# Splitting the attention of three token tiles around an expert gather, in a two-layer kernel on one Trainium2 core

## The chip, the cores and the metric

The kernel runs on one core of one Trainium2 chip. The metric is device time in microseconds (us) from the first to the last instruction of one execution, as the median of several runs. The core's engines are named as in the profile: PE is TensorE's matmul, PEld its weight load, DVE is VectorE, ACT is ScalarE, POOL is GpSimd, SP is SyncE; the core has 16 DMA engines, which SP's loads and POOL's gathers share.

## The reference

512 tokens of width 1024 in f32 pass through two layers. What matters here, cut down:

```python
def first_block(x, ...):
    h = rmsnorm(x, norm1_g)
    qa, ka, va, qb, kb, vb, ga, gb = split(h @ w_in)
    ya = neighbourhood_attention(qa, ka, va, rpb)      # 8 heads of 64
    yb = gqa_attention(rope(norm(qb)), rope(norm(kb)), vb)
    merged = sigmoid(ga) * (ya @ w_proj_a) + sigmoid(gb) * (yb @ w_proj_b)
    x = x + merged @ w_out
    x = x + peer(rmsnorm(x, norm2_g), peer_w_q, peer_sub_keys, peer_u, peer_v)
    return rmsnorm(x, norm_f_g)

def peer(xn, w_q, sub_keys, u, v):
    # per token: 8 heads, top 16 of 128 keys on two sides, top 16 of their sums:
    # 128 experts of 16384, each a row of u and a row of v
    act = einsum("cd,ced->ce", xc, u[ic])
    hid = gelu(act) * gate
    return einsum("ce,ced->cd", hid, v[ic])

def second_block(x, ...):      # a state-space layer over the sequence, in order
    ...
```

Each token picks 128 experts, and each expert is 8 KB (1024 values of u, 1024 of v). For 512 tokens that is 512 MB of rows read by index, against some 170 MB of weights.

## The kernel before

The tokens are four tiles of 128 (0 to 3), one token per partition. The order of work is written by hand and then list-scheduled by the framework, which keeps dependences.

**Front.** Keys and values of all tokens; then attention, gates and merge of tile 0 alone (`mix_first`), then tile 0's expert queries and choices (`queries`, `ranked`).

**The gather.** `peers` is a generator. One step of it handles two experts of the current tile (a pair). For each expert, POOL issues one indirect DMA that brings 128 rows of 8 KB (1 MB) into a buffer `g` (six buffers, line 269); DVE multiplies the u half with the token and sums it (L271); ACT applies gelu (L276); DVE puts act times gate on a diagonal `dg` (L280); PE multiplies `dg` with the v half, in 64 x 64 quarters of its array, into two accumulators (L285). For tile 0 both experts of a pair share one gelu and one visit of PE, PE takes only the left half of v, and DVE adds up the right half in a buffer `own` (L295). A tile has 64 pairs; the four tiles have 256. At the end of a tile `folded` adds the accumulators to the residual `xres` and leaves `pre[t]`.

**Beside it.** `Paced` wraps PE: each matmul counts its columns (times 4 for f32), and whenever the count passes `every`, one step of `peers` is emitted. So other PE work and gather pairs alternate: one pair per 13600 columns (`PACE_B`) during `mix_rest([1, 2, 3])` (attention, gates `ga`/`gb`, merge `pj`/`xo` of the other three tiles at once, with 384 columns per matmul) and during the queries of tile 1; one per 10500 (`PACE_Q`) during the queries of tiles 2 and 3; then the choices of tiles 2 and 3 on DVE, with `steps_now(3)` after each head; then, once tile 1 is folded, one per 4600 (`PACE_C`) during the second layer of tiles 0 and 1 (`block_c([0, 1])`). What is left of the gather is drained, and `block_c([2, 3])` ends the kernel.

**Choices.** `top8` and `best` find the experts on DVE. `best` writes the indices `hk_idx[t]`; a pair cannot be gathered before its indices exist. `rows` and `cols` load a weight tile of 512 KB from SP for every 8 matmuls of a stage, whatever the number of token columns; four such tiles are in flight (`wp`). The bias tables `nab` of the attention are loaded per call of `mixers`, as wide as its tiles need.

Of the kernel before, what the change touches and what calls it, by code (L numbers as in the profile page):

```python
# [8 lines left out]
F32 = mybir.dt.float32  # L9
# [5 lines left out]
OP = mybir.AluOpType  # L15
# [5 lines left out]
NT = 4  # L21
# [152 lines left out]
def program(tc, a, out):  # L174
# [3 lines left out]
    first, rest = [0], [1, 2, 3]  # L178
    NG = 256
    PACE_B, PACE_Q, PACE_C = 13600, 10500, 4600  # L180

    with ExitStack() as ctx:
# [40 lines left out]
        folds = [two[:, 1:3, :], two[:, 0:2, :]]  # L223
# [21 lines left out]

        def peers(gp, lp):
# [5 lines left out]
            for t in range(NT):  # L252
# [7 lines left out]
                for e0 in range(0, P, 2):  # L260
                    while len(hk_idx[t]) < e0 + 2:
                        yield
                    gs = []
                    grp = 2 if t == 0 else 1
                    for j in range(2):
                        if j % grp == 0:
                            act = sm.tile([P, 2], F32, tag="act", name="act", bufs=4)
                        g = gp.tile([P, 2, D], F32, tag="g", name="g")
                        G.indirect_dma_start(out=g.rearrange("p a d -> p (a d)"), out_offset=None, in_=a["uv"],  # L269
                                             in_offset=bass.IndirectOffsetOnAxis(ap=hk_idx[t][e0 + j], axis=0))  # L270
                        V.scalar_tensor_tensor(g[:, 0, :], g[:, 0, :], 1.0, xnp, op0=OP.mult, op1=OP.mult,  # L271
                                               accum_out=act[:, j % grp:j % grp + 1])
                        gs.append(g)
                        if (j + 1) % grp:
                            continue
                        A.activation(act[:, :grp], act[:, :grp], AF.Gelu)  # L276
                        gate = hk_gate[t][:, e0 + j + 1 - grp:e0 + j + 1]
                        dg = dgs()
                        for m in range(grp):
                            V.tensor_scalar(dg[:, m, :], two[:, 1, :], act[:, m:m + 1], gate[:, m:m + 1], op0=OP.mult, op1=OP.mult)  # L280
                        for m in range(2):
                            for i in range(2):
                                r, o = slice(64 * i, 64 * i + 64), slice(64 * m, 64 * m + 64)
                                w, v = (dg[r, m, :], gs[m][r, 1, HALVES[0]]) if grp == 2 else (dg[r, 0, :], g[r, 1, HALVES[m]])
                                T.tensor.matmul(acc[i][o, :], w, v, start=(e0 + j + 1 == grp), stop=(e0 + j + grp >= P),  # L285
                                                tile_position=(64 * i, 64 * m), skip_group_check=True)
                    if t == 0:
                        hid = sm.tile([P, 2], F32, tag="hid", name="hid", bufs=4)
                        V.tensor_tensor(hid, act, gate, op=OP.mult)
                        for j, g in enumerate(gs):  # L290
                            if own is None:
                                own = gp.tile([P, 512], F32, tag="own", name="own", bufs=1)
                                V.tensor_scalar(own, g[:, 1, HALVES[1]], hid[:, 0:1], None, op0=OP.mult)
                            else:
                                V.scalar_tensor_tensor(own, g[:, 1, HALVES[1]], hid[:, j:j + 1], own, op0=OP.mult, op1=OP.add)  # L295
                    if parts is not None:
                        folded(t - 1, parts, done[1])
                        parts = None
                    yield
                done = acc, own  # L300

            A.activation(col("rt"), act[:, 0:1], AF.Sqrt, bias=eps, scale=0.0)
# [11 lines left out]
        def folded(t, parts, own):  # L314

            acc = [bank("fold", "sb")] + ([bank("fold", "sb")] if own is None else [own])
            for i in range(2):
                if own is None:
                    for k in range(2):
                        r, o = slice(64 * k, 64 * k + 64), slice(64 * i, 64 * i + 64)  # L320
                        T.tensor.matmul(acc[k][o, :], two[r, 1, :], parts[r, i, :], start=True, stop=True,
                                        tile_position=(64 * k, 64 * i), skip_group_check=True)
                else:
                    T.tensor.matmul(acc[0], folds[i].rearrange("p a b -> p (a b)"), parts[:, i, :], start=(i == 0), stop=(i == 1))
# [3 lines left out]
            for k, h in enumerate(HALVES):  # L328
                V.tensor_tensor(xt[:, h], xt[:, h], acc[k], op=OP.add)
                A.activation(acc[k], xt[:, h], AF.Square, accum_out=ss[:, k, 0:1])  # L330
# [56 lines left out]
        with pool("pa") as pa:  # L387
# [28 lines left out]
            with pool("ph") as ph:  # L416
# [76 lines left out]
                def mix_rest(tiles, hs):  # L493
                    n = len(tiles) * P
                    with pool("p2") as py:
# [9 lines left out]
                        def spread(u):  # L505

                            if u < 8:
                                gate(u, a["wga"], mT)
                            if 12 <= u < 20:
                                if not gb:  # L510
                                    gb.append(pa.tile([P, 8, n], F32, tag="kv", name="gb"))
# [632 lines left out]
```

## Time and profile before

| | us |
|---|---|
| median of 3 runs | 2219.3 (2218.5 to 2221.38) |
| profiled execution, its own time | 2217.67 |
| its span | 2215.8 |
| PE busy | 1851.5 |
| DVE busy | 1628.1 |
| ACT busy | 735.1 |
| POOL busy | 598.8 |

The span runs from the first to the last instruction; 1.9 us lie around it. Busy times of engines overlap. The mean granted TensorE clock is 0.887. HBM reads are 707.67 MB. A window row of the profile gives, for a stretch in us from the span's start, the busy time of each engine, PE's granted clock, the DMA engines' mean busy share and the GB/s that they moved.

### The profile page before, as it was taken

Reading aid. Unit: us, or ns where it says so; the run is one execution under the profiler, and the core shown is the slowest. Engines: PE = TensorE matmul, PEld = TensorE weight load, DVE = VectorE, ACT = ScalarE, POOL = GpSimd, SP = SyncE. Lnnn points to the kernel's source line nnn. Section 1 sums busy time; section 2 is a strip of 40 time slices with the busy share of each in tenths; the row PEclk is TensorE's granted clock in tenths of the full one; section 3 lists DMA queues with packets and bytes.
Section 4 is the critical chain, followed back from the end, with each engine's and each line's share of the span. In section 5 each row is a group of like instructions: output and inputs, shape, how many; then the busy total and the mean of one; then the engine's idle time right before and its main releaser. Section 6 shows DMA issues by size and latency. Waiting matters only on the chain.

```text
span 2215.8 us, 29509 instructions
## 1 busy us (share of the span) xinstructions
PE 1851.5 (84%) x10292; PEld 1032.5 (47%) x10292; DVE 1628.1 (73%) x4007; ACT 735.1 (33%) x1471; POOL 598.8 (27%) x520
## 2 busy tenths in 40 slices
PE   7998699899999898656648886896899866799998
PEld 5767445444444654001104552462453421298896
DVE  5376986788885966888868887886775766687865
ACT  4374265566501421111123342321220310154443
POOL 0000223333331233444433334433423333200000
PEclk9999789999999998656758997998999976699999
DMA  5366979889997899999989989899999999653363
GB/s 211 127 228 216 363 288 344 335 325 350 346 381 273 316 378 394 380 380 397 362 306 346 418 365 396 335 418 420 406 415 416 402 416 421 276 170 97 119 189 121
DMA packets 127316, 711.71 MB, mean 321 GB/s; under 512 B 15168, under 2 KB 18752, under 8 KB 61248
## 3 DMA queue, kind: packets, MB, share of 16 engines
q0 software_dynamic: 73728, 536.90, 60.6%
q1 hardware_dynamic: 53440, 172.92, 22.1%
q8 instruction: 83, 1.36, 0.2%
q14 instruction: 65, 0.53, 0.1%
HBM read 707.67 MB, written 2.10 MB: 320 GB/s over the span
## 4 chain that ended last, share of the span: by engine, by line
PE 36%; DMA 25%; DVE 24%; issue 7%; ACT 6%; POOL 1%; another core or an unknown queue 0%; DVEq 0%; POOLq 0%; ACTq 0%; SPq 0%
DMA g<-in_uv,idx 23%; DVE g L271 9%; PE sc L168 5%; PE acc L285 4%; PE mix L168 3%; PE pq L168 2%; PE ga L168 2%; PE z L168 2%; DVE dg L280 2%; PE pg L168 2%; PE ys L168 2%; DVE ww L354 2%; POOL g L269 1%; DVE own L295 1%; PE xbc L168 1%
## 5 line engine op out<-in xcount | busy, mean ns | idle before, releaser
L269 POOL DMA_INDIRECT g<-in_uv,idx x512 | 595.0, 1162 | 1297.7 <-PE acc L285 610.2
L285 PE MATMUL acc<-g,dg 64*64 64x512 f32 x3584 | 626.5, 755 | 249.9 <-DVE dg L280 229.8
L271 DVE SCALAR_TENSOR_TENSOR g<-g,xnp 128x1024 f32<-128x1024 f32 x512 | 624.7, 1221 | 188.2 <-DMA g<-in_uv,idx 181.9
L285 PEld LDWEIGHTS acc<-g,dg 64*64 64x64 f32 x3584 | 122.9, 154 | 621.0 <-DVE dg L280 492.8
L276 ACT ACTIVATE act<-act 128x1 f32<-128x1 f32 (+1 forms) x448 | 90.8, 203 | 945.7 <-DVE g L271 912.2
L354 DVE TENSOR_TENSOR ww<-w,ww 128x1024 fp32r<-128x1024 f32 x175 | 213.4, 1222 | 76.4 <-ACT ww L353 74.5
L280 DVE TENSOR_SCALAR dg<-two,act,gate 128x64 f32<-128x64 f32 x512 | 172.1, 351 | 132.6 <-ACT act L276 129.9
L353 ACT CAST ww<-w 128x1024 fp32r<-128x1024 f32 x175 | 182.2, 1044 | 172.8 <-PE sc L168 63.6
L168 PEld LDWEIGHTS sc<-hT,ww 128*128 128x128 f32 x1536 | 190.0, 193 | 54.0 <-issue 44.5
L168 PE MATMUL sc<-hT,ww 128*128 128x256 f32 x1536 | 206.1, 289 | 6.0 <-ACT fold L333 3.2
L168 PE MATMUL pq<-xT,w 128*128 128x128 f32 (+1 forms) x768 | 127.8, 323 | 0.6 <-DMA w<-in_wq 0.6
L168 PEld LDWEIGHTS pq<-xT,w 128*128 128x128 f32 x768 | 112.0, 200 | 19.8 <-issue 12.2
L295 DVE SCALAR_TENSOR_TENSOR own<-g,hid,own 128x512 f32<-128x512 f32 x127 | 95.1, 749 | 2.3
L168 PE MATMUL ga<-h,w 128*128 128x384 f32 x256 | 93.1, 513 | 2.8 <-DVE rot L411 2.8
L276 ACT ACT_TABLE_LOAD x61 | 78.3, 1283 | 18.1 <-DVE g L271 16.3
L168 PE MATMUL xbc<-hT,ww 128*128 128x256 f32 x480 | 64.2, 290 | 6.2 <-DVE ww L354 3.3
L168 PEld LDWEIGHTS xbc<-hT,ww 128*128 128x128 f32 x480 | 59.3, 192 | 20.4 <-issue 9.5
L168 PEld LDWEIGHTS ga<-h,w 128*128 128x128 f32 x256 | 48.7, 198 | 37.6 <-issue 8.3
L168 PE MATMUL q<-h,w 128*128 128x128 f32 (+1 forms) x256 | 61.1, 394 | 3.4 <-ACT rsq L407 3.4
L168 PE MATMUL mix<-w,ycat 128*128 128x512 f32 x128 | 61.5, 612 | 0.0
L168 PEld LDWEIGHTS z<-hT,ww 128*128 128x128 f32 x384 | 46.9, 190 | 12.3 <-issue 10.5
L168 PE MATMUL z<-hT,ww 128*128 128x256 f32 x384 | 50.5, 287 | 1.5 <-ACT raw L928 1.3
(338 smaller groups left out, 2269.8 us busy)
## 6 DMA issues: line engine op xcount, KB each, us to landing
w<-in_w SPq DMA_DIRECT2D x100, 512.0 KB
w<-in_wq SPq DMA_DIRECT2D x48, 512.0 KB
w<-in_wo SPq DMA_DIRECT2D x32, 512.0 KB
w<-in_wgm SPq DMA_DIRECT2D x16, 512.0 KB
w<-in_wout SPq DMA_DIRECT2D x16, 512.0 KB
g<-in_uv,idx POOLq DMA_INDIRECT x512
w<-in_wpg SPq DMA_DIRECT2D x16, 512.0 KB
w<-in_wqa SPq DMA_DIRECT2D x8, 512.0 KB
```

The lines of the kernel that those rows point to most:

```text
L168: return self.count(max(n, 128) * (4 if rhs.dtype == F32 else 1), self.tensor.matmul(out, lhsT, rhs, **kw))
L269: G.indirect_dma_start(out=g.rearrange("p a d -> p (a d)"), out_offset=None, in_=a["uv"], in_offset=bass.IndirectOffsetOnAxis(ap=hk_idx[t] ...
L271: V.scalar_tensor_tensor(g[:, 0, :], g[:, 0, :], 1.0, xnp, op0=OP.mult, op1=OP.mult, accum_out=act[:, j % grp:j % grp + 1])
L276: A.activation(act[:, :grp], act[:, :grp], AF.Gelu)
L280: V.tensor_scalar(dg[:, m, :], two[:, 1, :], act[:, m:m + 1], gate[:, m:m + 1], op0=OP.mult, op1=OP.mult)
L285: T.tensor.matmul(acc[i][o, :], w, v, start=(e0 + j + 1 == grp), stop=(e0 + j + grp >= P), tile_position=(64 * i, 64 * m), skip_group_chec ...
L295: V.scalar_tensor_tensor(own, g[:, 1, HALVES[1]], hid[:, j:j + 1], own, op0=OP.mult, op1=OP.add)
L353: A.copy(ww[:, 0], w)
L354: V.tensor_tensor(ww[:, 1], w, ww[:, 0], op=OP.subtract)
```

## The change

`mix_rest` is called twice: for tiles 1 and 2, and later for tile 3. After the first call come the queries of tiles 1 and 2 together, with tile 1's choices made at once and tile 2's scores kept. After the second call come tile 3's queries. The choices of tiles 2 and 3 are a list `side` of small functions (one per head, one per `best` of four heads); `peers` runs one of them after every third pair. In `peers` each expert has its own gelu and its own visit of PE; for tile 0 PE takes both halves of v of every even expert and the left half of every odd one, and DVE adds up the right half of the odd ones only. The three paces change. The gates are spread over the attention units by a rule that depends on the number of tiles. The pools `pk` (choices) and the place of `gb` are new.

```diff
-    first, rest = [0], [1, 2, 3]
+    first, late = [0], [2, 3]
     NG = 256
-    PACE_B, PACE_Q, PACE_C = 13600, 10500, 4600
+    PACE_B, PACE_Q, PACE_C = 11300, 6400, 5200
...
-                for e0 in range(0, P, 2):
-                    while len(hk_idx[t]) < e0 + 2:
+                for e in range(P):
+                    while len(hk_idx[t]) <= e:
                         yield
-                    gs = []
-                    grp = 2 if t == 0 else 1
-                    for j in range(2):
...
-                        A.activation(act[:, :grp], act[:, :grp], AF.Gelu)
-                        gate = hk_gate[t][:, e0 + j + 1 - grp:e0 + j + 1]
-                        dg = dgs()
-                        for m in range(grp):
-                            V.tensor_scalar(dg[:, m, :], two[:, 1, :], act[:, m:m + 1], gate[:, m:m + 1], op0=OP.mult, op1=OP.mult)
-                        for m in range(2):
-                            for i in range(2):
-                                r, o = slice(64 * i, 64 * i + 64), slice(64 * m, 64 * m + 64)
-                                w, v = (dg[r, m, :], gs[m][r, 1, HALVES[0]]) if grp == 2 else (dg[r, 0, :], g[r, 1, HALVES[m]])
-                                T.tensor.matmul(acc[i][o, :], w, v, start=(e0 + j + 1 == grp), stop=(e0 + j + grp >= P),
-                                                tile_position=(64 * i, 64 * m), skip_group_check=True)
-                    if t == 0:
-                        hid = sm.tile([P, 2], F32, tag="hid", name="hid", bufs=4)
-                        V.tensor_tensor(hid, act, gate, op=OP.mult)
-                        for j, g in enumerate(gs):
...
-                                V.scalar_tensor_tensor(own, g[:, 1, HALVES[1]], hid[:, j:j + 1], own, op0=OP.mult, op1=OP.add)
...
+                    V.scalar_tensor_tensor(g[:, 0, :], g[:, 0, :], 1.0, xnp, op0=OP.mult, op1=OP.mult, accum_out=act)
+                    A.activation(act, act, AF.Gelu)
+                    dg = dgs()
+                    V.tensor_scalar(dg[:, 0, :], two[:, 1, :], act, hk_gate[t][:, e:e + 1], op0=OP.mult, op1=OP.mult)
+                    aside = t == 0 and e % 2 == 1
+                    for k in range(1 if aside else 2):
+                        for i in range(2):
+                            r, o = slice(64 * i, 64 * i + 64), slice(64 * k, 64 * k + 64)
+                            last = P - 2 if k and t == 0 else P - 1
+                            T.tensor.matmul(acc[i][o, :], dg[r, 0, :], g[r, 1, HALVES[k]], start=(e == 0), stop=(e == last),
+                                            tile_position=(64 * i, 64 * k), skip_group_check=True)
+                    if aside:
+                        hid = sm.tile([P, 1], F32, tag="hid", name="hid", bufs=4)
+                        V.tensor_tensor(hid, act, hk_gate[t][:, e:e + 1], op=OP.mult)
...
+                            V.scalar_tensor_tensor(own, g[:, 1, HALVES[1]], hid, own, op0=OP.mult, op1=OP.add)
+                    if e % 2:
+                        if parts is not None:
+                            folded(t - 1, parts, done[1])
+                            parts = None
+                        if side and e % 6 == 1:
+                            side.pop(0)()
+                        yield
...
-                            if u < 8:
-                                gate(u, a["wga"], mT)
-                            if 12 <= u < 20:
...
-                                gate(u - 12, a["wgb"], gb[0])
+                            each = 2 if len(tiles) == 1 else 1
+                            kind, v = divmod(u, 4 * len(tiles))
...
+                            for i in range(each * v, min(each * v + each, 8)):
+                                gate(i, a["wgb" if kind else "wga"], gb[0] if kind else mT)
...
                 T.beside(peers(gp, lp), PACE_B)
-                mix_rest(rest, h2)
-        late = rest[1:]
-        with pool("p4") as pw:
-            with pool("p5") as pq:
-                queries(pq, rest[:1], [(h, 2, rest[:1]) for h in (0, 2, 4, 6)], lambda *x: ranked(pw, *x))
-            T.every = PACE_Q
...
-            with pool("p5") as pq:
-                queries(pq, late, [(h, 2, late) for h in (0, 2, 4, 6)], after)
-
-            for t in late:
-                for h in range(8):
...
-                    T.steps_now(3)
-            while 1 not in pre:
-                T.steps_now(1)
-            T.every = PACE_C
+                mix_rest([1, 2], h2[:, :, 0:2 * P])
+                pk = pick.enter_context(pool("pk", side="right"))
...
+                def choices(t):
+
+                    for h in range(0, 8, MOST):
+                        f = []
+                        for m in range(MOST):
+                            side.append(lambda f=f, h=h, m=m: part(t, f, h, m))
+                        side.append(lambda f=f, h=h: best(pk, t, f, h, MOST))
+
+                with pool("p3") as pw:
+                    queries(pw, [1, 2], [(h, 2, [1, 2]) for h in (0, 2, 4, 6)], after)
+                T.every = PACE_Q
+                choices(2)
+                mix_rest([3], h2[:, :, 2 * P:])
+        with pool("p5") as pq:
+            queries(pq, [3], [(h, 2, [3]) for h in (0, 2, 4, 6)], after)
+        choices(3)
+        while side:
+            T.steps_now(1)
+        pick.close()
+        while 1 not in pre:
+            T.steps_now(1)
+        T.every = PACE_C
```

`after` ranks tile 1's heads at once and copies the scores of tiles 2 and 3 to a kept tile; `part` copies two rows of scores and runs `top8` on them. `folded` takes tile 0's second half as two 64 x 64 products more and one DVE addition of `own`.

## Rows read from the trace of the kernel before

**Rows 1.** The page: span, DMA busy tenths and GB/s in 40 slices, the ending chain by line.

```profile
span 2215.8 us, 29509 instructions
...
DMA  5366979889997899999989989899999999653363
GB/s 211 127 228 216 363 288 344 335 325 350 346 381 273 316 378 394 380 380 397 362 306 346 418 365 396 335 418 420 406 415 416 402 416 421 276 170 97 119 189 121
...
DMA g<-in_uv,idx 23%; DVE g L271 9%; PE sc L168 5%; PE acc L285 4%; PE mix L168 3%; PE pq L168 2%; PE ga L168 2%; PE z L168 2%; DVE dg L280 2%; PE pg L168 2%; PE ys L168 2%; DVE ww L354 2%; POOL g L269 1%; DVE own L295 1%; PE xbc L168 1%
```

**Rows 2.** Windows: stretch, its us, busy by engine (instructions), PE clock, DMA share, GB/s.

```profile
225.00:700.00 475.00, 427.83 (x1896) 208.41 (x1896) 380.60 (x969) 213.72 (x378) 147.27 (x127) 0.94 0.88 338
700.00:741.00 41.00, 39.78 (x305) 35.30 (x304) 24.03 (x142) 10.89 (x26) 1.51 (x2) 1.00 0.78 257
741.00:765.00 24.00, 14.41 (x69) 10.21 (x67) 19.41 (x95) 15.35 (x26) 4.21 (x6) 0.79 0.93 372
...
765.00:875.00 110.00, 101.49 (x572) 60.22 (x568) 70.14 (x211) 25.89 (x72) 39.53 (x35) 0.96 0.95 374
875.00:1135.00 260.00, 153.95 (x724) 25.31 (x728) 221.95 (x739) 38.67 (x135) 113.83 (x91) 0.63 0.95 377
1135.00:1215.00 80.00, 54.22 (x325) 26.92 (x318) 56.08 (x121) 20.46 (x53) 25.12 (x22) 0.80 0.85 317
1215.00:1780.00 565.00, 487.92 (x3040) 254.29 (x3042) 425.31 (x871) 157.53 (x347) 210.31 (x179) 0.93 0.99 400
1780.00:1915.00 135.00, 88.35 (x444) 16.60 (x436) 84.49 (x159) 13.60 (x56) 52.07 (x51) 0.72 1.01 419
```

**Rows 3.** Timeline of POOL, 676 to 765: gathers by start, us, idle before and releaser.

```profile
683.95 1.50 POOL L269 DMA_INDIRECT g<-in_uv,idx  x1 [0.30 <-issue]
...
739.19 0.94 POOL L269 DMA_INDIRECT g<-in_uv,idx  x1 [53.74 <-issue]
...
745.40 0.94 POOL L269 DMA_INDIRECT g<-in_uv,idx  x1 [0.30 <-issue]
764.90 0.94 POOL L269 DMA_INDIRECT g<-in_uv,idx  x1 [18.57 <-DVE idxf L789]
```

**Rows 4.** Groups by line, 225 to 700: count, busy us, mean ns, idle before, releasers.

```profile
L285 PE MATMUL acc<-g,dg 64*64 64x512 f32 x512 | 87.5, 650 | 23.6 <-DVE dg L280 22.9 <-DVE hid L289 0.7
...
L168 PE MATMUL pq<-xT,w 128*128 128x128 f32 x87 | 13.6, 323 | 0.0
L168 PE MATMUL sc<-subk,q 128*128 128x128 f32 x16 | 4.3, 384 | 2.6 <-ACT q L715 2.6
...
L295 DVE SCALAR_TENSOR_TENSOR own<-g,hid,own 128x512 f32<-128x512 f32 x127 | 95.1, 749 | 2.3
L276 ACT ACT_TABLE_LOAD x34 | 43.6, 1283 | 0.6
```

**Rows 5.** Groups by line and shape, the whole span: PE's query products.

```profile
L168 PE MATMUL pq<-xT,w 128*128 128x128 f32 x512 | 64.5, 284 | 0.6 <-DMA w<-in_wq 0.6
L168 PE MATMUL pq<-xT,w 128*128 128x256 f32 x256 | 63.3, 401 | 0.0
```

**Rows 6.** Windows of the gather's accumulators alone (PE, PEld, DVE, ACT).

```profile
765.00:875.00 110.00, 38.65 (x276) 8.76 (x272) 0.00 (x0) 0.00 (x0) 0.96 0.95 374
```

**Rows 7.** Timeline of PE, 333 to 339: start, us, instructions merged.

```profile
334.22 1.07 PE L285 MATMUL acc<-g,dg 64*64 64x512 f32 x4
335.22 0.66 PE L171 MATMUL pT<-idn,s 128*128 128x128 f32 x4
335.81 1.93 PE L285 MATMUL acc<-g,dg 64*64 64x512 f32 x12
```

**Rows 8.** Windows: a stretch with weights and gathers, one with gathers alone, one of choices.

```profile
1215.00:1315.00 100.00, 89.25 (x691) 60.09 (x693) 87.27 (x198) 40.17 (x81) 36.19 (x30) 1.00 1.02 419
...
1835.00:1895.00 60.00, 40.43 (x196) 6.74 (x192) 38.80 (x73) 4.86 (x24) 24.25 (x24) 0.68 1.01 421
...
975.00:1015.00 40.00, 23.83 (x116) 3.99 (x112) 35.97 (x123) 6.43 (x21) 17.34 (x13) 0.60 0.88 335
```

**Rows 9.** DMA queues: packets, MB, time of their packets as a share of 16 engines.

```profile
q0 software_dynamic: 73728, 536.90, 60.6%
q1 hardware_dynamic: 53440, 172.92, 22.1%
```

More of the change, by code (lines that the diff above doesn't have):

```diff
@@ L244, in program @@
         hk_idx, hk_gate, hk_f = {}, {}, {}
+        side = []
         def peers(gp, lp):
@@ L314, in folded @@
         def folded(t, parts, own):
-            acc = [bank("fold", "sb")] + ([bank("fold", "sb")] if own is None else [own])
+            acc = [bank("fold", "sb") for _ in range(2)]
             for i in range(2):
[L318 to L324, printed above, removed]
+                for k in range(2):
+                    r, o = slice(64 * k, 64 * k + 64), slice(64 * i, 64 * i + 64)
+                    T.tensor.matmul(acc[k][o, :], two[r, 1, :], parts[r, i, :], start=True, stop=True,
+                                    tile_position=(64 * k, 64 * i), skip_group_check=True)
             xt = xres[:, t, :]
@@ L329, in folded @@
                 V.tensor_tensor(xt[:, h], xt[:, h], acc[k], op=OP.add)
+                if k and own is not None:
+                    V.tensor_tensor(xt[:, h], xt[:, h], own, op=OP.add)
                 A.activation(acc[k], xt[:, h], AF.Square, accum_out=ss[:, k, 0:1])
@@ L505, in spread @@
                         def spread(u):
[L507 to L512 removed]
+                            each = 2 if len(tiles) == 1 else 1
+                            kind, v = divmod(u, 4 * len(tiles))
+                            if kind and not gb:
+                                last = tiles[-1] == NT - 1
+                                gb.append((pa if last else py).tile([P, 8, n], F32, tag="kv" if last else "gb", name="gb"))
+                            for i in range(each * v, min(each * v + each, 8)):
+                                gate(i, a["wgb" if kind else "wga"], gb[0] if kind else mT)
                         def put(i, b):
@@ new lines, in program, with after, part @@
+                pk = pick.enter_context(pool("pk", side="right"))
+                kept = {}
+                def after(t, h0, nh, b):
+                    if t == 1:
+                        return ranked(pk, t, h0, nh, b)
+                    if h0 == 0:
+                        kept[t] = pk.tile([P, 16, P], F32, tag="kept", name="kept")
+                    A.activation(kept[t][:, 2 * h0:2 * (h0 + nh), :], b, AF.Copy, scale=xn[t])
+                def part(t, f, h, m):
+                    if not f:
+                        f += firsts(pk, f"{h}")
@@ L836, in program @@
                     for j in range(2):
                         sc = dgs().rearrange("p a b -> p (a b)")
[L838 to L845 removed]
+                        A.copy(sc, kept[t][:, 2 * (h + m) + j, :])
```

40 lines of the change are left out of this document (11 added, 29 removed).

## The prediction

> **What bounds the kernel now.** I read the page first, then windows cut where the work changes, then POOL's timeline where the GB/s dip, then the groups by line of the stage that the change rearranges.
>
> The page shows the gather everywhere: the ending chain goes through it more than through anything else (23% DMA, 9% the DVE product behind it), and the 16 engines are nearly full from slice 5 to slice 34 while the rate is not constant: about 340 GB/s early, 415 and more later [rows 1]. The finer windows give the ceiling. With weights and gathers together and DVE 87% busy the core moves 419 GB/s; with gathers alone 421 [rows 8]. So 420 GB/s is what the DMA engines give here, whoever asks. Everything below it between the first gather (225 us) and the last (about 1915) is loss, and it has four places [rows 2]:
>
> - 225 to 700, 338 GB/s. This is the mix of tiles 1 to 3 beside tile 0's gather. PE is busy 427.8 of 475 us at clock 0.94. PE sets the pace here, not DMA.
> - 700 to 765. Tile 0's gathers are all issued at 684; POOL then sits idle for 53.7 us, issues six (all buffers) from 739 to 745, and waits again 18.6 us for the first later one at 764.9 [rows 3]. Tile 1's indices do not exist earlier, because its queries follow the merge of all three tiles. This hole in the gather is bridged only by weights (257 GB/s from 700 to 741).
> - 765 to 1215, 374, 377 and 317 GB/s: queries (PE busy 101.5 of 110), the choices of tiles 2 and 3 on DVE (222 of 260 us busy, PE's clock 0.63), and the change to the second layer.
> - 1215 to 1780, 400 GB/s, then 419 to the end of the gather: nearly at the ceiling.
>
> After 1915 comes the second layer of tiles 2 and 3, which the diff does not touch.
>
> So the end of the gather plus a constant is the time. I carry the sum to that point, against the profiled execution: span 2215.8, its own time 2217.7, which is 1.6 us below the median of the runs.
>
> **Part 1, until tile 1's queries are through.** Before, their last product ends at 741. Four things change.
>
> *Work leaves.* In 225 to 700 PE is busy 427.8 us, less 87.5 for the gather, 13.6 and 4.3 for the rest of tile 0's queries [rows 2, 4]: 322.4 us for three tiles of mix. Tile 3's third, 107.5 us, moves out.
>
> *Work comes in.* Tile 2's queries now run with tile 1's. A pass of two tiles costs 63.3 us, one of a single tile 64.5/2 = 32.2 [rows 5], so 31 us more; its scores add 16 f32 products, 32 records, at 4.3 us per 16 [rows 4]: 9. Together 40.
>
> *The pair is cut in two.* Tile 0's 64 pairs cost 87.5 us of PE, 1.37 each [rows 4]. An expert with all four quarters costs 38.65/34.5 = 1.12 us (276 records, eight to an expert) [rows 6]. The odd expert, with two of the quarters, is not in the trace as such. It costs at least half, 0.56, and at most the same 1.12. The nearest row is a visit of four records that holds PE from 334.22 to 335.22, 1.00 us [rows 7]; I take that. The new pair is 2.12, 0.75 more, times 64 is 48 us (ends: 20 and 56).
>
> The Trainium skill, "TensorEngine Tiling (Array Packing)", Key Properties, says that a change of tiling mode drains the engine, which speaks against the change, since each expert is now a visit of its own between 128 x 128 products. The trace agrees in so far as the short visit above shows 1.00 us and not 0.56; at the rule's worst the sum would stand 8 us higher, at my upper end.
>
> *DVE is relieved.* 64 fewer additions of 749 ns, 48 us of 404.6 busy. PE is idle 48 us from 225 to 741, of which 22.9 wait for `dg` on DVE [rows 2, 4]. I give back a third of that, 8 us (ends 0 and 23). The extra 64 gelus lie on ACT, which is busy 213.7 of 475; they bring at most as many table loads again as now, 34 for 43.6 us [rows 4], under the same cover. `folded`'s extra addition for tile 0 is one DVE instruction. Neither is counted.
>
> 741 - 107.5 + 40 + 48 - 8 = 713.5 (ends 670 and 730). Does tile 0's gather fit? By the counts in `Paced` the mix of two tiles and their queries have 688 thousand columns, 61 pairs at 11300; before, 799 thousand at 13600 call for 59 and all 64 were done by 700 (512 records [rows 4]), so the schedule runs about five ahead. It fits, and tile 1's first choices come a quarter of the way through the queries, so the hole has no reason to return. At 713.5 the gather is therefore where it was at 764.9, with 134 issued: **51 us of lead**.
>
> **Part 2, more bytes.** `mix_rest` loads 40 weight tiles of 512 KB per call whatever its width: 4 + 4 queries, 8 + 8 gates, 8 projections, 8 outputs. Called twice, that is 21.0 MB more. The bias tables are 640 and 512 columns instead of 768, 8 of each: 1.6 MB more. Also, by 765 the old kernel already holds some six weight tiles of the queries of tiles 2 and 3, 3.1 MB. At 420 GB/s the 25.6 MB cost **61 us** of DMA time. Priced by SP's own queue (22.1% of 2215.8 us for 172.92 MB, 2.83 us per MB [rows 9]) they cost 73.
>
> The Trainium skill, "DMA: Bandwidth & Descriptors", Issuing engines are not separate DMA queues, says that DMAs of all issuers end on the same 16 engines, so SP's loads would not ride free beside POOL's gathers. Here 419 with both against 421 with gathers alone agrees [rows 8]. If they rode free, the sum below would be 61 us lower.
>
> **Part 3, what is lost against 420 GB/s afterwards.** Before, bytes over 420 against the length of each window gives 12, 27, 20, 27 and 0 us lost in the last five stretches [rows 2], 86 in all. After:
>
> - Tile 3's mix and queries at 6400 columns per pair are 344 thousand columns, 54 pairs. They move 113 MB of experts and 33 MB of weights and tables, 347 us at the ceiling, 6.4 us per pair. PE needs (107.5 + 32 + 9)/54 + 2 x 1.12 = 5.0 us per pair and is no longer the bound. Tile 2's choices run beside it, three pairs per function. The nearest row with weights, gathers and a busy DVE loses nothing (419); the farthest is the present choice stage at 377, which would lose 36. I take 5, near the first, because weights keep flowing while DVE is in a burst.
> - Tile 3's choices alone: 30 pairs instead of 48 for two tiles, half of 27, 13 us. The burst of `best` stays: with DVE busy 36 of 40 us the rate falls to 335 GB/s [rows 8].
> - The change to the second layer 20, the second layer 27, as before; its DMA-bound pairs do not care that the pace is 5200 and not 4600.
>
> 65 in place of 86: **21 us back**. Where the choices leave the empty stage, their cover is the DMA time of the weights; without that cover they cost the 36.
>
> **Sum.** -51 + 61 - 21 = -11 us. Span 2205, own time 2207, and by the 1.6 us between it and the median, 2209.
>
> **Rivals.**
>
> *The visits are cheap (faster).* If the odd expert costs half and DVE's relief removes all 22.9 us of waiting, part 1 ends at 670 and the sum is -54, 2166. For it: the quarters of one expert do run together (1.12 for four, 1.37 for a pair). Against it: the 1.00 us visit [rows 7].
>
> *The second reading of the weights is not absorbed (slower).* In tile 3's stage the gathers go on losing at the rate of the present choice stage, since the same DVE bursts hold the six buffers, and the weights cost their own queue's price: 31 + 12 us more, sum +32, **2251**. Place: the some 350 us after part 1. It decides there: 146 MB in 347 + 16 us is 402 GB/s; below that mean the change is no gain. For it: 374 and 377 GB/s in the two stages before 1135 [rows 2]. Against it: 419 with DVE at 87% [rows 8].
>
> *Part 1 gains nothing (no change).* One gelu per expert among the exponentials and tanhs doubles the table loads; if their 43.6 us stand in the chain from DVE to PE in place of behind it, about a quarter reaches PE, 11 us, and the sum is 0: 2219. For it: each load is 1.28 us between a product and its `dg`. Against it: ACT idle half of the time.
>
> **How the numbers follow.** About 0.2%, 4.4 us, can be told from no change. I give the forecast 0.40 (its own range 2194 to 2224: 0.25 faster, 0.09 same, 0.06 slower), cheap visits 0.19, unabsorbed weights 0.33, no gain in part 1 0.08. Faster 0.25 + 0.19 = 0.44, same 0.09 + 0.08 = 0.17, slower 0.06 + 0.33 = 0.39. The terms nearly cancel, so the sign is weakly held. The range leaves a tenth on each side: 2172 (not quite the cheap visits in full) to 2254 (the unabsorbed weights with little beyond).
>
> **What would show it.** POOL's idle 53.7 us gone, tile 1's gathers following tile 0's without a gap; PE's gather time for tile 0 about 136 us instead of 87.5; the last product of the joint queries near 714; a stage of tile 3's mix above 402 GB/s; the weight queue at about 195 MB; the end of the gather some 11 us earlier; the second layer of tiles 2 and 3 as long as now. The prediction is wrong if the joint queries end after 730, if tile 3's stage stays under 400 GB/s, or if the second layer of tiles 0 and 1 is not through when the gather ends, so that the last part starts later than its data.

## The result and the profile after

The changed kernel takes 2296.66 us (median of 4 runs, 2294.41 to 2302.15) against 2219.12 for the kernel before beside it: ratio 1.0351, interval 1.0331 to 1.0371. It is 3.5% slower; the forecast was 2209 and its range ended at 2254. The profiled execution took 2302.15 us, 84.5 more than the profiled one of the kernel before (2217.67); the medians differ by 77.5. Sums by stage, below, are taken from the profiles.

The page after (span, DMA tenths, GB/s in 40 slices, weight queue):

```profile
span 2300.4 us, 31324 instructions
...
DMA  5366978797989888999998899969999999843363
GB/s 204 124 229 225 394 271 349 280 348 303 387 314 386 318 339 339 393 417 416 379 376 337 325 419 395 370 225 419 412 416 416 417 378 422 364 129 115 119 183 119
...
q1 hardware_dynamic: 60352, 195.47, 23.9%
```

The weight queue moved the forecast 195 MB [rows 9]. Early, the rate did not rise: slices five to fourteen lie between 271 and 394, where those of the kernel before lie between 273 and 381 [rows 1]. To see where the time lies I cut at 765, as in [rows 2], and at the last gather's issue, with the columns of [rows 2]. First the two stretches of the kernel before:

```profile
225.00:765.00 540.00, 482.02 (x2267) 253.92 (x2266) 424.04 (x1205) 239.95 (x430) 152.99 (x134) 0.94 0.87 333
765.00:1907.50 1142.50, 882.00 (x5070) 382.63 (x5066) 853.28 (x2088) 255.55 (x660) 439.67 (x377) 0.83 0.97 388
```

Then the changed kernel; 735 and 1080 are where the joint queries and tile 3's queries end:

```profile
225.00:735.00 510.00, 458.50 (x2243) 263.40 (x2242) 355.91 (x1101) 204.99 (x412) 140.81 (x128) 0.93 0.86 334
...
225.00:765.00 540.00, 482.59 (x2350) 275.12 (x2350) 385.09 (x1222) 213.83 (x437) 148.47 (x134) 0.92 0.87 336
765.00:1996.40 1231.40, 977.25 (x5808) 457.70 (x5804) 874.89 (x2096) 324.65 (x773) 453.88 (x377) 0.84 0.94 380
...
735.00:1080.00 345.00, 289.80 (x1826) 152.78 (x1824) 233.65 (x704) 121.09 (x278) 109.83 (x94) 0.91 0.94 370
1080.00:1996.40 916.40, 711.55 (x4090) 316.64 (x4090) 670.42 (x1512) 212.39 (x520) 351.71 (x290) 0.82 0.94 383
...
760.00:940.00 180.00, 155.53 (x962) 80.49 (x962) 137.77 (x457) 95.39 (x194) 53.33 (x47) 0.87 0.87 331
940.00:1080.00 140.00, 115.17 (x771) 63.01 (x770) 71.70 (x148) 18.18 (x66) 48.84 (x41) 0.96 1.02 417
```

The last gather is issued at 1996.4 instead of 1907.5 (89 us later); what follows is as long as before (304 and 308 us), as forecast. So all of the loss lies between 225 us and the gather's end. There I keep the prediction's account: a stretch of d us at r GB/s moves d x r and loses d x (1 - r/420). Up to 765 the kernel before lost 112 us, the changed one 108; after 765 it lost 87 (388 GB/s over 1142.5 us), now 117; and 26 MB more were moved, 63 us at 420 GB/s. -4 + 30 + 63 = 89. The forecast was -51 - 21 + 61 = -11.

The first stage by groups of lines, 225 to 735, where the joint queries end (last score product at 734.2):

```profile
L277 PE MATMUL acc<-g,dg 64*64 64x512 f32 x732 | 146.0, 651 | 31.1 <-DVE dg L271 28.2 <-DVE hid L281 1.4 <-DVE idx L787 1.3
L168 PE MATMUL ga<-h,w 128*128 128x256 f32 x256 | 68.0, 418 | 0.0
```

At 12 records a pair, 732 records are 61 pairs, 2.39 us each; before it was 1.37 [rows 4]. Single visits in PE's timeline show why; each 64 x 64 product shows as two records (`x8` is four products). The profile models where a matmul ends, but the start of the next product is recorded, so I go by that:

```profile
303.45 1.09 PE L277 MATMUL acc<-g,dg 64*64 64x512 f32 x8
304.47 0.43 PE L168 MATMUL y<-pT,kv 128*64 128x128 f32 x2
...
330.29 1.08 PE L277 MATMUL acc<-g,dg 64*64 64x512 f32 x4
331.30 0.66 PE L171 MATMUL pT<-idn,s 128*128 128x128 f32 x4
...
761.95 1.97 PE L277 MATMUL acc<-g,dg 64*64 64x512 f32 x4
```

Eight records, on four quarters of the array, hold PE 1.02 us (303.45 to 304.47), four records, on two quarters, 1.01: the odd expert costs a whole visit for half the products. The granted clock is 1.00 in both. The last row is the same visit at the lower of PE's two clock levels, 1.2 GHz:

```profile
758.00:766.00 8.00, 8.00 (x21) 3.08 (x19) 8.00 (x33) 3.22 (x11) 0.00 (x0) 0.50 0.55 216
```

The hole in the gather is gone, as forecast: POOL's longest wait between 600 and 1000 is 16.73 us, at 673, where 53.74 stood [rows 3].

```profile
673.35 0.94 POOL L266 DMA_INDIRECT g<-in_uv,idx  x1 [16.73 <-DVE i L724]
```

### The profile page after: what moved, and what is told of

Read it like the earlier page. It is cut to its first block, busy times and chain, and to the rows that moved or that the text cites. A ratio compares the mean times of both kernels' runs of the same rounds, so it can differ in the third digit from the quotient of the medians.

```text
span 2300.4 us, 31324 instructions
## 1 busy us (share of the span) xinstructions
PE 1939.9 (84%) x11080; PEld 1122.2 (49%) x11080; DVE 1604.8 (70%) x4004; ACT 776.5 (34%) x1587; POOL 607.1 (26%) x520
## 4 chain that ended last, share of the span: by engine, by line
PE 31%; DMA 28%; DVE 21%; issue 9%; ACT 8%; POOL 2%; SPq 0%; POOLq 0%; DVEq 0%; ACTq 0%
DMA g<-in_uv,idx 24%; DVE g L268 9%; PE sc L168 5%; PE acc L277 3%; PE ga L168 2%; PE z L168 2%; PE mix L168 2%; POOL g L266 2%; PE ys L168 2%; PE pq L168 2%; ACT L269 2%; DVE dg L271 2%; PE xbc L168 1%; DVE ww L347 1%; PE pg L168 1%
## 5 line engine op out<-in xcount | busy, mean ns | idle before, releaser
L266 POOL DMA_INDIRECT g<-in_uv,idx x512 | 603.3, 1178 | 1377.2 <-PE acc L277 770.7
L277 PE MATMUL acc<-g,dg 64*64 64x512 f32 x3840 | 679.3, 723 | 261.7 <-DVE dg L271 236.7
L269 ACT ACTIVATE act<-act 128x1 f32<-128x1 f32 x512 | 103.7, 203 | 1002.6 <-DVE g L268 981.3
L277 PEld LDWEIGHTS acc<-g,dg 64*64 64x64 f32 x3840 | 137.1, 149 | 604.4 <-DVE dg L271 450.1
L271 DVE TENSOR_SCALAR dg<-two,act,gate 128x64 f32<-128x64 f32 x512 | 182.7, 357 | 161.2 <-ACT act L269 159.8
L168 PE MATMUL ga<-h,w 128*128 128x256 f32 (+1 forms) x512 | 104.6, 355 | 0.0
L168 PEld LDWEIGHTS ga<-h,w 128*128 128x128 f32 x512 | 82.9, 202 | 27.0 <-issue 19.7
L168 PE MATMUL q<-h,w 128*128 128x128 f32 (+1 forms) x384 | 70.2, 338 | 5.5 <-ACT rsq L401 5.5
L168 PEld LDWEIGHTS q<-h,w 128*128 128x128 f32 x384 | 60.3, 211 | 27.6 <-issue 13.4
L168 PE MATMUL pj<-yT,w 128*128 128x256 f32 (+1 forms) x256 | 49.6, 343 | 4.1 <-DVE mT L673 2.0
```

Of the source, the lines that this page charges most:

```text
L168: return self.count(max(n, 128) * (4 if rhs.dtype == F32 else 1), self.tensor.matmul(out, lhsT, rhs, **kw))
L269: A.activation(act, act, AF.Gelu)
L271: V.tensor_scalar(dg[:, 0, :], two[:, 1, :], act, hk_gate[t][:, e:e + 1], op0=OP.mult, op1=OP.mult)
L277: T.tensor.matmul(acc[i][o, :], dg[r, 0, :], g[r, 1, HALVES[k]], start=(e == 0), stop=(e == last), tile_position=(64 * i, 64 * k), skip_gr ...
```

## The experiments

Fourteen kernels ran, in four groups, each beside the kernel before (medians 2216.8 to 2220.5). The diffs are cut and shortened to what matters. The first four ask whether the pairs or the bytes cost the time.

**e1: the changed schedule, the pairs of before.**

```diff
-  for e in range(P):            # own gelu and visit per expert
+  for e0 in range(0, P, 2):     # before's pairs and own; folded as before
+      if side and e0 % 6 == 0: side.pop(0)()
```

> The changed kernel's schedule with tile 0's pairs as they were (one gelu and one PE visit per pair, left half of v on PE, right half on DVE). Theory V (separate visits): tile 0's gather costs PE 155 us in the changed kernel against 87.5 before; with the pairs back the joint queries end near 700 instead of 758 and the kernel takes 2235 us (2225 to 2250) instead of 2297. Rival B (bytes): the DMA engines set the time in every stage, the first included, and the pairs matter little: 2285 to 2300.

Measured: 2237.51, ratio 1.0108 (1.0080 to 1.0136). 59 of the 77 us go with the pairs alone. The joint queries end at 638.4, not near 700; the changed kernel's end at 735 (not at the 758 that the expectation names). PE's pairs from 225 to 638:

```profile
L287 PE MATMUL acc<-g,dg 64*64 64x512 f32 x424 | 70.5, 652 | 24.8 <-DVE dg L282 24.8
```

These are 53 pairs, where the changed kernel has 61 ahead of the same point: the framework's list scheduling orders the work anew, so e1 differs from the changed kernel in that order, too. Of the 96 us some 75 are the pairs' time on PE (146.0 less 70.5).

The gathers show where the pairs' cost comes out. Here are the last ones of tiles 0 and 1, in e1 and then in the changed kernel:

```profile
706.59 0.94 POOL L271 DMA_INDIRECT g<-in_uv,idx  x1 [0.30 <-DVE v L734]
1117.99 0.94 POOL L271 DMA_INDIRECT g<-in_uv,idx  x1 [1.04 <-DVE v L734]
```

```profile
732.05 1.11 POOL L266 DMA_INDIRECT g<-in_uv,idx  x1 [0.30 <-DVE rf L768]
1180.85 1.97 POOL L266 DMA_INDIRECT g<-in_uv,idx  x1 [1.74 <-PE acc L277]
```

The changed kernel is 25 us behind at the end of tile 0's gather, 63 at the end of tile 1's, and 69 at the last gather (1927.0 and 1996.4). So over half of the delay arises in tile 1's gather, whose pairs are the same in both. That PE, 96 us late, still has tile 3's mix to do there is the likely reason; it was not tried by itself.

**e2: the schedule and paces of before, the changed pairs and `folded`.**

```diff
-  for e0 in range(0, P, 2):     # in the kernel before
+  for e in range(P):            # own gelu and visit per expert, six products a pair
```

> The kernel before with only the per-expert visits of the change (and its folded), old schedule, old paces. Theory V: the first stage is bound by PE and grows by what the visits cost, 45 to 68 us, and the hole behind it stays: 2262 to 2287 us. Rival B: the visits cost nothing that shows, DVE's relief pays for them: 2211 to 2228.

Measured: 2303.48, ratio 1.0386 (1.0369 to 1.0404), 87 us over its 2216.81 and 16 over theory V's upper end. Two windows, three short ones, and two groups of 225 to 800:

```profile
225.00:765.00 540.00, 477.48 (x2080) 220.38 (x2079) 340.72 (x906) 237.28 (x451) 141.68 (x128) 0.90 0.77 294
765.00:2001.00 1236.00, 965.73 (x5532) 444.68 (x5530) 904.90 (x2333) 280.36 (x714) 450.28 (x383) 0.83 0.94 376
...
450.00:460.00 10.00, 4.57 (x24) 1.97 (x20) 7.33 (x12) 3.55 (x5) 4.01 (x4) 0.80 1.02 420
...
470.00:480.00 10.00, 7.38 (x41) 2.33 (x35) 7.28 (x18) 7.07 (x15) 6.62 (x5) 0.99 0.93 338
480.00:490.00 10.00, 10.00 (x13) 2.84 (x14) 6.88 (x17) 8.59 (x15) 0.93 (x1) 0.50 0.76 297
```

```profile
L276 PE MATMUL acc<-g,dg 64*64 64x512 f32 x768 | 154.1, 649 | 34.5 <-DVE dg L270 29.6 <-DVE hid L280 4.7
L168 PE MATMUL ga<-h,w 128*128 128x384 f32 x256 | 99.2, 542 | 0.5 <-DVE rot L401 0.5
```

The visits take 154.1 us for 87.5, 2.41 per pair: 67 us. The granted clock is 0.90 up to 765 (0.94 before). PE is idle for over half of 450 to 460 and for a quarter of 470 to 480; from 480 to 490 it is busy all through, at the lower level, 0.50. `ga` and `pj` grow from 93.1 and 44.0 to 99.2 and 49.5 us, 12 more. DVE is busy 341 of 540 us (424 before), and PE still waits 29.6 us for `dg`: a DVE with more free time did not make PE wait less. The hole stays (POOL idle 86.67 us before 834), for tile 1's indices are as late as they were.

**e3 and e4: fewer bytes.** Tile 3's mix loads an eighth of each weight tile (half for `wout`), 16.8 MB less; tile 3's mix is then another one. e3 is the changed kernel so, e4 is e1 so.

```diff
-  SP.dma_start(t, src)
+  SP.dma_start(t[:, 0:1, :], src[:, 0:1, :])   # in tile 3's mix
```

> The changed kernel, but the second call of the mix (tile 3) loads one eighth of each 512 KB weight tile (one half of an output tile) and uses that slice for all, so 16.8 MB of the 21 MB read twice are not moved and tile 3's mix is not the reference's. Theory B: 16.8 MB at 420 GB/s are 40 us, at the queue's own price 47: 2250 to 2260 us. Theory V: the stage is not bound by DMA, loads fill gaps: 2285 to 2297.

> Both: old pairs for tile 0 and the short loads in tile 3's mix (so tile 3's mix is not the reference's). If V and B each hold for their own part and add up: 2297 - 60 - 43 = 2194 us (2180 to 2215), below the kernel before. If one of them is only a shift of waiting from one stage to another, the two together give little more than the larger alone: 2235 to 2255.

Measured: 2271.10 (1.0251, 1.0225 to 1.0277) and 2233.04 (1.0066, 1.0047 to 1.0085): 26 and 4.5 us less than with all bytes, where 16.8 MB at 420 GB/s are 40. e3 lies between its two theories, e4 just under its second; e4's 4.5 us are no more than the spread of its runs (2228 to 2235) and e1's (2231 to 2248). After 765 e4 runs at 380 GB/s where e1 has 389:

```profile
765.00:1929.50 1164.50, 909.24 (x5458) 425.03 (x5456) 833.75 (x1959) 271.68 (x687) 438.28 (x366) 0.85 0.94 380
```

With fewer weights to move, the gather fills only part of the room. Bytes are one limit among several, and their price is not additive.

The second group splits the dearer pair and looks for what else holds e1 above the kernel before.

**e5: the kernel before, a gelu and a visit per expert, same eight records.**

```diff
-  for m in range(2): ...            # one visit for the pair
+  for m in (j,): ... dg[r, 0, :], g[r, 1, HALVES[0]]   # per expert j, column half j
```

> The kernel before, where tile 0's two experts of a pair no longer share a gelu and a visit of TensorE: each has its own, of two products into one column half. Products, bytes, VectorE's own sums and the whole schedule stay. Theory 'separate visits cost': a pair that comes as two visits between other work takes about 2 us of TensorE instead of 1.37 although nothing is multiplied more, so the first stage grows by 35 to 60 us and the time is 2250 to 2280. Rival 'only the third pair of products costs': the same eight records cost what they cost before, the first stage ends within 10 us of before, 2215 to 2228.

**e6: the kernel before, one visit per pair, six products, the changed `folded`; DVE adds only the odd right half.**

```diff
-  for m in range(2): ... w, v = dg[r, m, :], gs[m][r, 1, HALVES[0]]
+  for x, m in ((0, 0), (0, 1), (1, 0)): ... w, v = dg[r, x, :], gs[x][r, 1, HALVES[m]]
```

> The kernel before, where tile 0's pairs keep one gelu and one visit of TensorE but have the changed kernel's six products (both halves of the even expert, the left half of the odd one) and VectorE adds up the odd one's right half alone. Theory 'separate visits cost': the two products more cost half a visit, 0.5 to 0.6 us per pair, 32 to 40 us of TensorE, and 64 additions of 0.75 us leave VectorE: 2235 to 2255. Rival 'the products cost all of it': the first stage grows by the 86 us that both together showed, 2290 to 2305. If this and the kernel with own visits each stand some 40 us over before, the two causes add up to what the changed pairs cost.

Measured: e5 2251.55 (1.0153, 1.0108 to 1.0198), e6 2282.58 (1.0298, 1.0263 to 1.0333). PE's group of tile 0's pairs, up to 765, in e5 and then in e6 (225 to 800):

```profile
L277 PE MATMUL acc<-g,dg 64*64 64x512 f32 x512 | 114.4, 648 | 29.8 <-DVE dg L273 25.7 <-DVE hid L282 3.9
```

```profile
L285 PE MATMUL acc<-g,dg 64*64 64x512 f32 x768 | 150.1, 642 | 22.3 <-DVE dg L280 19.6 <-DVE hid L290 2.3 <-issue 0.3
```

e6 loses what PE's row gains: 62.6 us of PE (150.1 - 87.5), 62 of time. e5 has 27 us more PE and loses 31. So the half-empty third pair of products, not the second visit, is the larger part: 2.35 us per pair in e6, against 1.79 for the old eight records in two visits. My expectation for e6 (half a visit for half the products) fell; e5 came at the low end of its first theory.

In e5 the two experts write different column halves; in e6 the odd expert's products go to quarters that the even one has just used. The timelines show what that does. Here are unbroken visits at a granted clock of 1.00, each with the next product: e5, e6, and the kernel before.

```profile
422.83 1.09 PE L277 MATMUL acc<-g,dg 64*64 64x512 f32 x8
423.85 1.13 PE L168 MATMUL s<-kv,qT 64*128 64x512 f32 x4
```

```profile
460.59 1.93 PE L285 MATMUL acc<-g,dg 64*64 64x512 f32 x12
462.46 1.13 PE L168 MATMUL s<-kTb,qT 64*128 64x512 f32 x4
```

```profile
511.92 1.95 PE L285 MATMUL acc<-g,dg 64*64 64x512 f32 x16
513.80 0.91 PE L168 MATMUL hss<-rsq,bd 128*128 128x384 f32 x2
```

e5's two experts, where they come together, hold PE 1.02 us, as long as one of them alone. e6's twelve records hold it 1.87 and sixteen of the kernel before 1.88. So the third pair of products adds some 0.85 us, as much as four products on all quarters, and over 64 pairs that is 54 of e6's 62.6 us. e6's mean is above 1.87 in part because the list scheduling cuts many of its pairs into two visits, and because some run at the lower clock.

e6 also tells what own gelus do. It has e2's products and additions but one gelu per pair, and PE waits 19.6 us for `dg`; in e2, with a gelu and a visit per expert, 29.6; before, 22.9 [rows 4]. Their times are 21 us apart.

**e7: e1 without tile 1's choices** (tile 1 takes tile 0's experts and gates).

```diff
-  return ranked(pk, t, h0, nh, b)
+  n = 16 * (h0 + nh)
+  hk_gate[1] = hk_gate[0]
+  hk_idx[1] = hk_idx[0][:n]
+  return
```

> The changed kernel's schedule with the pairs of before, where tile 1 takes tile 0's experts and gates, so that none of tile 1's choices are made on VectorE (tile 1's experts are then not the reference's; the bytes are the same). Theory 'tile 1's choices, which lay in the hole of the gather before, now stand in the way of tile 0's gather': without them 20 to 35 us are gone, 2202 to 2218 against 2237.5 with them. Rival 'TensorE paces that stage alone': the time stays within 8 us of 2237.5.

Measured: 2233.78 (1.0060, 1.0042 to 1.0079), 4 us below e1, or 7 when each is set against the kernel before beside it (2220.48 and 2216.81). The rival holds, at most a few us beside it: the 20 to 35 us of the theory are not there.

**e8: the kernel before with five gather buffers.**

```diff
-  pool("gp", 6, side="right")
+  pool("gp", 5, side="right")
```

> The kernel before with five gather buffers instead of six, nothing else. Theory 'the loop of gather, product, gelu, diagonal and TensorE visit through the buffers sets the rate in the stages below 420 GB/s': a sixth less in flight costs 5 to 15% there, and the time grows by 40 to 120 us. Rival 'TensorE or the DMA engines set the rate': under 12 us more, below 2232.

Measured: 2272.25 (1.0219, 1.0189 to 1.0248), 52 us: the theory holds for the total, but not stage by stage. The last gathers of tiles 0 and 1, in e8 and then tile 1's in the kernel before:

```profile
738.28 1.05 POOL L269 DMA_INDIRECT g<-in_uv,idx  x1 [7.51 <-DVE oh L780]
1161.35 1.92 POOL L269 DMA_INDIRECT g<-in_uv,idx  x1 [3.31 <-DVE rf L773]
```

```profile
1115.87 1.15 POOL L269 DMA_INDIRECT g<-in_uv,idx  x1 [2.83 <-PE acc L285]
```

Tile 0's gather ends 54 us late (683.95 before [rows 3]), tile 1's 45, the last 61 (1968.6 and 1907.5). So the sixth buffer is worth its time beside the mix of tiles 1 to 3; in tile 1's gather nothing more is lost, although that, too, ran below 420 GB/s before (374, 377 and 317 [rows 2]). What sets the difference was not tried.

The third group was formed from the windows of e1: after 765 it loses 86 us, 45 of them from 1215 to 1500, where the kernel before loses 22.

```profile
225.00:765.00 540.00, 466.25 (x2406) 285.68 (x2405) 454.55 (x1403) 225.89 (x432) 166.44 (x144) 0.91 0.93 364
...
1215.00:1500.00 285.00, 237.81 (x1544) 130.76 (x1545) 231.25 (x512) 88.08 (x186) 108.90 (x89) 0.88 0.90 354
...
765.00:1927.00 1162.00, 908.73 (x5457) 422.11 (x5456) 835.77 (x1949) 272.12 (x689) 436.71 (x366) 0.85 0.96 389
```

**e9: e1 with the second layer's pace back at 4600. e10: e1 with a step of the choices per two pairs. e11: both.**

```diff
-  PACE_B, PACE_Q, PACE_C = 11300, 6400, 5200
+  PACE_B, PACE_Q, PACE_C = 11300, 6400, 4600      # e9, e11
-  if side and e0 % 6 == 0:
+  if side and e0 % 4 == 0:                        # e10, e11
```

> The changed kernel's schedule with the pairs of before (2237.5 us), and the pace of the second layer back at one pair per 4600 columns instead of 5200. Theory 'the second layer's first 280 us are paced by TensorE, so the pace decides how many gathers fit': the 45 us that are lost there against 420 GB/s shrink to the 21 to 25 of before, the time is 2213 to 2226. Rival 'those losses come from short dependent products of the second layer, whatever the pace': within 8 us of 2237.5.

> The same schedule and pairs (2237.5 us), with one step of the list of choices after every second pair instead of every third. Theory 'tile 3's choices end too late and hold back the second layer': 10 steps come 10 pairs earlier, the second layer starts 25 to 50 us earlier than at 1244 and the time falls by 10 to 25 us, 2212 to 2228. Rival 'the start of the second layer does not matter, since the gather's bytes set the end': within 8 us of 2237.5; denser choices on VectorE may then cost up to 10.

> Both edits at once, pace 4600 and a step after every second pair. If the two act on different losses their gains add up and the time is 2200 to 2215, level with or below the kernel before; if they are two ways to the same loss, the time is that of the better one; if neither matters, 2230 to 2245.

Measured: e9 2217.77 (0.9996, 0.9980 to 1.0012), e10 2246.06 (1.0122, 1.0078 to 1.0167), e11 2230.32 (1.0040, 1.0018 to 1.0061). The pace is worth 20 us here. e10's second layer does start 26 us earlier (first `xbc` product at 1217.93 instead of 1244.46), and the time gets no better: 8.5 us more than e1. e11 is 12.5 us over e9, so the denser choices cost a little at either pace and the two do not add up. The windows of e9, the last three by stages of the work (638 and 988 are its ends of the joint queries and of tile 3's):

```profile
225.00:765.00 540.00, 469.37 (x2428) 288.75 (x2426) 457.56 (x1422) 226.87 (x436) 167.72 (x145) 0.92 0.93 365
...
1215.00:1500.00 285.00, 237.83 (x1597) 128.48 (x1597) 238.95 (x533) 88.80 (x193) 113.55 (x96) 0.90 0.95 380
...
765.00:1901.10 1136.10, 891.20 (x5440) 414.81 (x5440) 824.75 (x1935) 267.23 (x683) 434.89 (x366) 0.85 0.97 394
...
225.00:638.00 413.00, 377.05 (x1921) 239.98 (x1920) 342.00 (x1028) 168.06 (x318) 127.21 (x111) 0.95 0.94 368
638.00:988.00 350.00, 276.70 (x1779) 151.95 (x1777) 258.69 (x793) 117.44 (x274) 116.25 (x100) 0.90 0.96 380
988.00:1901.10 913.10, 706.83 (x4170) 311.62 (x4170) 681.62 (x1538) 208.60 (x526) 359.16 (x302) 0.83 0.97 394
```

From 1215 to 1500 POOL issues 96 gathers instead of 89.

The fourth group asks whether the pace is a price of its own: **e12** is the kernel before at 5200, **e13** the changed kernel at 4600, **e14** e1 at 4000.

```diff
-  PACE_B, PACE_Q, PACE_C = 13600, 10500, 4600
+  PACE_B, PACE_Q, PACE_C = 13600, 10500, 5200     # e12
-  PACE_B, PACE_Q, PACE_C = 11300, 6400, 5200
+  PACE_B, PACE_Q, PACE_C = 11300, 6400, 4600      # e13; 4000 in e14
```

> The kernel before with one number changed: the second layer of tiles 0 and 1 lets a pair through per 5200 columns instead of 4600. Theory 'the pace alone, in either schedule, is worth some 20 us': 2232 to 2244. Rival 'the pace matters only where the second layer starts late, as in the changed schedule': 2215 to 2226.

> The changed kernel as it is, with the pace of the second layer back at 4600 (2296.7 us with 5200). Theory 'visits and pace are separate prices that add up': 15 to 25 us less, 2272 to 2282. Rival 'with the dearer visits the gather has fallen so far behind that the end of the gather follows the bytes left': within 8 us of 2296.7.

> The changed kernel's schedule with the pairs of before and a pair per 4000 columns in the second layer (2217.8 us with 4600, 2237.5 with 5200). If the second layer's first part still has room for gathers, another 5 to 15 us are gone, 2203 to 2213, below the kernel before. If at 4600 the losses left come from elsewhere, within 5 us of 2217.8; a denser gather may also push the second layer back and cost a few us.

Measured: e12 2233.51 (1.0065, 1.0040 to 1.0091), e13 2295.36 (1.0342, 1.0298 to 1.0386), e14 2230.32 (1.0055, 1.0034 to 1.0077). The pace costs about 15 us in the schedule of before, too; in the changed kernel nothing that these runs can tell from zero (e13's interval reaches some 10 us to either side). e14 is 12.5 us slower than e9, more than any outcome named for it: of the three paces tried with the pairs of before, 4600 is the best. In the changed kernel the last gathers, changed kernel and then e13, are:

```profile
1996.41 0.94 POOL L266 DMA_INDIRECT g<-in_uv,idx  x1 [1.41 <-PE acc L277]
```

```profile
1978.18 0.94 POOL L266 DMA_INDIRECT g<-in_uv,idx  x1 [2.36 <-PE acc L277]
```

The gather ends 18 us earlier at 4600, but the rest of the span grows from 304 to 314 us; e9 against e1 shows the same, 315 and 303. Why the last layer takes longer after a denser gather was not tried. No version here beats the kernel before; e9 is level with it.

## Why the prediction was wrong

**Part 1, end of the joint queries.** Forecast 713.5, measured 735 (before 741). The terms can be set side by side. PE's work other than the pairs was forecast as 312.5 us (488.5 less 40 idle and 136 of pairs) and is 458.5 - 146.0 = 312.5: tile 3's third out and tile 2's queries in were right, taken together. The pairs were to take 136 us and took 146.0 for the 61 done by then; tile 0's 64, at 2.4, take about 153. PE idle was to fall to 40 us and is 51.5. 10 + 11.5 is the 21.5 us that are missing.

So two steps failed. First, the pair: I took 2.12 us, it is 2.39. The odd expert's 1.00 us was right (1.01 in the visit above); what the sum left out is that some visits run at the lower level, 1.97. An estimate: each visit weighted by the clock granted in it, the 146.0 us are 134 at full clock, 2.20 a pair, where the two visits above are 2.17. Second, the 8 us of DVE's relief: PE's waits for `dg` rose from 22.9 to 28.2 us although 64 additions left DVE. The relief with one gelu per pair shows as 3 us (e6: 19.6); with a gelu and a visit per expert the wait is 10 us more (e2: 29.6), and the prediction had put the second gelu at nothing ("Neither is counted").

The Trainium skill, "TensorEngine Tiling (Array Packing)", Key Properties, has the change of tiling mode drain the engine. I priced that at 8 us more at worst; e5, where the same records come in twice as many visits, shows 27 us of PE. That agrees in sign and is over three times my figure. But e5 also has two quarters filled in a visit instead of four, and the visits above put most of it there: four records alone hold PE as long as eight. An estimate from them: eight records hold 1.02 us and eight more 0.86, so a visit has some 0.16 us of its own, 10 us for 64 visits more. Whether this is the drain, no run here shows.

**Part 1, the lead.** Of the 51 us 4 came. I had 64 pairs and the first of tile 1 issued when the queries end, because the schedule ran five pairs ahead before. It did not: 61 pairs are through at 735, as the pace alone says, and 134 gathers are issued by 765, as many as before when its next went out at 764.90 [rows 3]. In losses up to 765 the lead is 112 less 108. With the pairs of before it is 40 us (112 against 72). So the hole was worth filling, and the dearer pairs ate nearly all of it.

**Part 2.** 25.6 MB and 61 us at 420 GB/s were right as an amount: 26 MB came. As a price it holds only where DMA is the limit. e3 and e4 got 1.5 and 0.3 us back per MB (25.6 and 4.5 us for 16.8 MB), not 2.4, and the 0.3 can hardly be told from nothing.

**Part 3.** Forecast 21 us back, measured 30 lost. In the prediction's own stages it had 61 us lost until the joint queries end (112 less 51), 5 in tile 3's mix and queries and 60 after. The changed kernel loses 104, 41 and 81; e9 loses 51, 33 and 57. The step that failed here is the 5 us, taken "because weights keep flowing while DVE is in a burst". Tile 3's stage ran at 370 GB/s (331 from 760 to 940, then 417), well under the 402 that I had put as the point where the rival of unabsorbed weights decides. With the pairs of before it failed as well: e9's stage runs at 380. Since e9 is level all the same, this is no separate cause of the 77 us. The second step is "its DMA-bound pairs do not care that the pace is 5200": in e9 and e12 they do. Two of the three signs of being wrong came: the joint queries ended after 730 and tile 3's stage stayed under 400 GB/s.

**The schedule alone.** e9 is the change without its two dear parts, and there the sum is near: 41 us less lost up to 765 (forecast 51), 22 MB more, 51 us (61), 17 less lost after 765 (21): -7, and the gather does end 6 us earlier (1901.1). That is in part luck: the 28 us too many in tile 3's stage are nearly made up by 10 less in the first stage, 3 less in the last and 10 less for bytes. What remains is given back at the end. From e9 the changed pairs at that pace (e13) cost 78 us, and on the schedule of before (e2) 87: they are the cause. The pace is 15 to 20 us with the pairs of before; with the new ones it no longer shows.

**The rivals.** With pairs at the old price, cheaper than cheap visits asked for, e9 is at 2218 and not near 2166. Unabsorbed weights had the sign and its sign-post (under 402 GB/s), but e9 has the same weights and the sign-post, too, and is level; in the changed kernel they show beside the dear pairs (26 us in e3) and are not what sets it apart. "No gain in part 1" was the mechanism nearest to what happened, and I gave it 0.08; it came through PE and not through the table loads, which are 35 from 225 to 735 where 34 stood [rows 4]. My upper end of 56 us for the pairs was too low: 2.41 less 1.37, times 64, is 67.

## What to carry to other kernels

Price a visit to a partly filled array by its time on the engine, not by its number of products: half the quarters cost a whole visit here. If one engine paces a stage, take work off it or leave it alone; moving half of DVE's additions to PE, where PE was busy 427.8 of 475 us [rows 2], cost 62 us by itself (e6) and 78 to 87 with a gelu and a visit per expert, although DVE gained. And test each constant that a change touches by itself: the pace, one number in the diff, took 15 to 20 us and hid a schedule that was level.

## What the runs showed of the hardware

A visit of 64 x 64 products with four records holds PE 1.01 us at full clock and one with eight 1.02; twelve hold it 1.87 and sixteen 1.88. So with f32 and 512 columns, products on quarters not yet used in the visit came free here, and the first on a used quarter added 0.85. Six products per pair cost 2.35 us of PE in the mean in e6, where four cost 1.37. A sixth of the gather buffers is worth 52 us, most of it lost while tile 0's gather runs beside the mix. Taking weights away gave 1.5 us per MB in the changed kernel and 0.3, hardly to be told from nothing, with the pairs of before, although the DMA engines are 94 to 97% busy from 765 to the end of the gather.
